# Three moves in the order of a fused attention and MLP block on one Trainium2 core

## The chip, the cores and the metric

The kernel runs on one NeuronCore of a Trainium2 chip. It is one launch that computes a whole residual block. The metric is the device time of one launch in microseconds (us); lower is better. In the rows of the profile PE is TensorE, DVE VectorE, ACT ScalarE, POOL GpSimd, and SP the engine whose queue issues nearly all transfers. Each engine works through its own list of instructions in order and waits for the others by semaphores.

## The reference

One sequence of 512 rows of width 2048 goes through an attention of 16 heads and an MLP of 8192 hidden columns, all in float32:

```python
h  = RMSNorm(x)
[qa|ka|va|qb|kb|vb|f] = h @ W_in
oa = stick-breaking attention (8 heads, strictly causal, no positions)
ob = forgetting attention (8 heads, causal, cumulative log-forget bias)
x  = x + concat(headnorm(oa), headnorm(ob)) @ W_out
x  = x + relu(RMSNorm(x) @ W_up)^2 @ W_down
y  = RMSNorm(x)
```

In the stick-breaking heads a query's weights are `exp(log_beta + rest)`, where `rest` is a running sum over keys from the right, which the kernel computes with scans.

## The kernel before, in words

**Numbers.** A float32 product is made of three products of shorter floats. `split` (L63) writes a high part (`wh`, `ah`, `fh`, `vh`, `ph`), on ACT, and the rest as a low part (`wl`, `al`, `fl`, `vl`, `pl`), on DVE: L65 and L66, or with a scale L68 and L69, which only V uses. A matmul then comes as high by high (L98), low by high (L99) and high by low (L100). So most of the work of ACT and DVE is splitting, and PE needs both parts of a piece soon after one another.

**Stages.** From 0 to about 628 us the projections and the heads; to about 795 us the output projection; to about 821 us its end, together with the turning of its result for the MLP; to about 1447 us the up-projection; then the down-projection, and the last norm to 2071 us.

**Output projection.** It is a Strassen-like scheme of seven products, numbered 1 to 7, over the two halves of each side. Their left sides are sums and differences of quarters of the heads' outputs (`mixed`). `left(p, j)` makes the part of product p's left side for two heads: for 5 a sum (L281), for 6 a difference (L283), for 2, 3 and 7 differences in place (L285, L287), and then a split. In the rows `al` with `ah` numbers 5298, 5320, 5322, 5318 and 5883 belongs to the products 1, 2, 5, 6 and 7. `out_piece` loads a piece of the weights (`wraw`, from `in_w_out` or from the prepared `tw`) and splits it; `out_product` multiplies it: 12 matmuls to a piece, half of them into each of two banks (`acca`, later `accc`). `add` (L595) adds the banks to the residual `r`. The first products start before the last two heads are done: their matmuls lie between those of the last V (`accv`), of two heads' outputs `o` (weights `ph`, `pl`, the transposes `pt` of `w`, times `vh`, `vl`) and of the sums of squares `ssq`. `first_outputs` (L563) issues this stretch. The list of each engine comes from a scheduler: the order of issue in the code is a priority, and `issue_after` tells it to hold something until an instruction has its place. V's parts have the highest priority there.

**The end of the output projection** is written out by hand for ACT and DVE. `out_step(j)` runs the 12 matmuls of piece j of product 4, with pieces split ahead (`ahead`). `turn_block` stores a finished half of the residual, turns it by eight transposes on PE (`tr`) and scales it on ACT into `h`; `to_sum`, `to_high` and `to_low` make of it the MLP's left sides (`fh`, `fl`, numbers 1 to 7 again: 6257, 6259, 6850, 6261, 6542, 6263, 6265). `squares` sums for the norm.

**Up-projection.** It goes through 32 units of 256 hidden columns (`Unit`); each again has seven products of 2.8 us on PE, and a product is `split_part` (its weights, `wh` and `wl`, or `wx`), `multiply` (16 matmuls) and `close`. A unit has three banks: A (`psa`) for 1, 6, 7 and 4, one after the other, B (`psb`) for 2, C (`psc`) for 5 and 3. After 1, 6 and 7 ACT copies bank A (L925, `s`) before the next product may go on in it; DVE adds B or C and forms the hidden columns, which are split (`st`) and stored (`ufd`). The units whose number leaves 2, 5 or 7 when divided by 8 load raw quarters and make their sums on DVE (L890 to L895). The loop takes one unit (`new`) together with the end of the one before (`old`):

```python
for i, (who, p) in enumerate(((new, 1), (old, 4), (new, 5), (new, 6), (old, 3), (new, 2), (new, 7))):
```

Units 0 and 1 stand ahead of the loop, with single loads (`more`) and products written out.

Of the kernel before, what the change touches and what calls it, by code (L numbers as in the profile page):

```python
# [8 lines left out]
F32 = mybir.dt.float32  # L9
F32R = mybir.dt.float32r  # L10
AF = mybir.ActivationFunctionType
ALU = mybir.AluOpType
# [28 lines left out]
def block_kernel(ctx, tc, x, g_attn, w_in, b_f, g_out_sb, g_out_fox, w_out, g_mlp, w_up, w_down, g_final, y):  # L41
    nc = tc.nc
    pe, act, dve, pool, sp = nc.tensor, nc.scalar, nc.vector, nc.gpsimd, nc.sync
# [14 lines left out]
    acc_cm = tc.tile_pool(name="acc", bufs=4, space=PSUM)  # L58
    acc = acc_cm.__enter__()

    lows, casts, loads, scaled = [None], [None], [None], [None]

    def split(hi, lo, src, scale=None):  # L63
        if scale is None:
            ins = casts[0] = act.copy(hi, src)  # L65
            lows[0] = dve.tensor_tensor(lo, src, hi.bitcast(F32), op=ALU.subtract)  # L66
        else:
            ins = act.mul(hi, src, scale)  # L68
            scaled[0] = dve.scalar_tensor_tensor(lo, src, scale, hi.bitcast(F32), op0=ALU.mult, op1=ALU.subtract)  # L69
        return ins  # L70

    more_parts, turn = [], [0]
# [83 lines left out]
    def out_rows(half, j, n):  # L156
        e = order[NH * half + 2 * j]
        return w_out[e * P:(e + 2) * P, n * NT:(n + 1) * NT].rearrange("(a p) c -> p a c", p=P)
# [50 lines left out]
    with tc.tile_pool(name="att", bufs=1, side="right") as at:  # L209
# [50 lines left out]
        def out_piece(p, c, j):  # L260

            src = out_rows(p > 1, j, 2 * c + (p == 3)) if p < 4 else tw[c][j][:, {5: 0, 7: 1, 6: 2, 4: 3}[p]]
            raw_turn[0] += 1
            i = raw_turn[0] % (3 + len(spares))
            raw = wp.tile([P, 2, NT], F32, tag="wraw", name="wraw") if i < 3 else spares[i - 3]()
            loads[0] = sp.dma_start(raw, src)
            hi, lo = (wp.tile([P, 2, NT], F32R, tag=f"w{q}", name=f"w{q}") for q in "hl")
            split(hi, lo, raw)
            return hi, lo

        def left_tile(p, pool_):
            LT[p] = tuple(pool_.tile([P, NH, 2 * P], F32R, tag=f"f{q}{LEFT_AT[p]}", name=f"a{q}{p}") for q in "hl")

        def left(p, j, k=1):

            m0, m1 = late["mixed"]
            ks = slice(2 * j, 2 * (j + k))
            a11, a21, a12, a22 = (m[:, ks, i:i + 2 * P] for m in (m0, m1) for i in (0, 2 * P))
            s = late["s"][j] if p in (5, 6, 3) else None
            if p == 5:  # L280
                dve.tensor_tensor(s, a21, a22, op=ALU.add)  # L281
            if p == 6:
                dve.tensor_tensor(s, s, a11, op=ALU.subtract)  # L283
            if p == 7:
                dve.tensor_tensor(a21, a11, a21, op=ALU.subtract)  # L285
            if p == 3:
                dve.tensor_tensor(a12, a12, s, op=ALU.subtract)  # L287
            if p == 1 and j < 2:
                out = [at.tile([P, 2, 2 * P], F32R, tag=f"a{q}{j}", name=f"a{q}1") for q in "hl"]
                late[1, j] = out  # L290
            else:
                out = [LT[p][q][:, ks] for q in range(2)]
            split(*out, {1: a11, 2: a12, 5: s, 6: s, 3: a12, 7: a21, 4: a22}[p])
# [203 lines left out]
        with tc.tile_pool(name="attp", bufs=1, space=PSUM) as atp:  # L497
# [46 lines left out]
            def residual(h, n, tiles):  # L544

                for t in range(2):
                    sp.dma_start(tiles[t], xq[:, 2 * h + t, n * NT:(n + 1) * NT])
                return tiles

            def two(c, dt=F32):  # L550
                return [up.tile([P, NT], dt, tag=f"u{p}{c}", name="r") for p in "hl"]

            def load_mixed(k):
                sp.dma_start(late["mixed"][k // NH][:, k % NH, :], md[order[k]])

            def before_outputs():
# [3 lines left out]
                left(1, 0)  # L560
                left(1, 1)

            def first_outputs():  # L563
                for k in (2 * NH - 4, 2 * NH - 3):
                    load_mixed(k)
                hp_cm.__exit__(None, None, None)
                pool_ = ctx.enter_context(tc.tile_pool(name="form", bufs=1, reuse_waits="tile"))
                FP.update((p, pool_) for p in (5, 6, 7, 4))
                spares.append(lambda: at.tile([P, 2, NT], F32, tag="raw4", name="wraw"))
                left_tile(1, pool_)  # L570
                with tc.issue_after(scaled[0].ins):
                    left(1, 2, 2)
                late["A"] = [[acc.tile([P, NT], F32, tag="acc", name="acca") for _ in range(2)] for c in range(2)]
                late[1, 1, 0], late[1, 1, 1] = (residual(0, 2 * c, two(2 + c)) for c in range(2))
                late["s"] = [w.rearrange("p (a b) -> p a b", a=2) for c in range(2) for w in two(c)]
                for p in (6, 2, 5):
                    left_tile(p, pool_)
                for c in range(2):
                    for j in range(4):
                        yield from out_product(late["A"][c], 1, c, [j], True, True)  # L580
                        if c == 0 and j < 3:
                            left(5, j)
                            left(6, j)
                    add(late[1, 1, c], late["A"][c])
                for c in range(2):
                    for j in range(3):
                        yield from out_product(late["A"][c], 6, c, [j], False, False)
                        if c == 0 and j == 0:
                            left(2, 0, 2)
                        if c == 0 and j == 1:  # L590
                            left(2, 2)

            def add(r, ps):
                for t in range(2):
                    dve.tensor_tensor(r[t], r[t], ps[t], op=ALU.add)  # L595
# [77 lines left out]
    def turn_block(h, n, r):  # L673

        for t in range(2):
            sp.dma_start(xd[n][:, 2 * h + t, :], r[t])
        for q in range(2):
            tr = trp.tile([P, 2, 2 * P], F32, tag="tr", name="tr1")
            for t in range(2):
                for i in range(2):  # L680
                    pe.transpose(tr[:, i, t * P:(t + 1) * P], r[t][:, (2 * q + i) * P:(2 * q + i + 1) * P], ident)
            for i in range(2):
                k = 2 * q + i
                act.mul(H[h][:, n, k, :], tr[:, i, :], g_up[:, 4 * n + k:4 * n + k + 1])
# [122 lines left out]
    r21 = [residual(1, 2 * c, two(2 + c)) for c in range(2)]  # L807
    for c in range(2):
        form_tile(5, c)
    for j in range(4):  # L810
# [8 lines left out]
        if j == 3:  # L819
            for b in range(2):  # L820
                squares(1, 2 * b + 1, r22[b])
    ahead = {j: out_piece(4, 1, j) for j in range(2)}
    M1 = []
    GROUPS = [(0, 3), (3, 3)] + [(u, 4) for u in range(6, NU - 2, 4)]
    ufd, at_unit = {}, {}
# [222 lines left out]

    out_step(0)
    add(r21[0], A[0])  # L1050
    ahead[2] = out_piece(4, 1, 2)
    out_step(1)
    ahead[3] = out_piece(4, 1, 3)
    u0, u1 = Unit(0), Unit(1)
    u0.more(5)
    turn_block(1, 0, r21[0])
    to_sum(5, 0)
    to_high(5, 0)
    to_sum(7, 0)
# [6 lines left out]
    to_low(7, 0)  # L1066
    out_step(2)
    u0.split_part(2)
    u0.more(7)
    to_high(6, 0)  # L1070
    to_low(6, 0)
    to_high(4, 0)
# [9 lines left out]
    u0.open_banks()  # L1082
    u1.open_banks()
    u1.split_part(1)
    u1.more(5)
    for n in (1, 3):
        to_high(3, n)
        to_low(3, n)
# [21 lines left out]
    to_high(4, 2)  # L1110
    to_low(4, 2)
    u1.multiply(2)
    u0.split_part(7)
    for n in (0, 2):
        to_high(3, n)
        to_low(3, n)
# [1 line left out]
    u1.close(2)  # L1118
    squares(1, 2, r21[1])
    u0.multiply(5)  # L1120
    u1.split_part(5)
    both_cm.__exit__(None, None, None)
    mixp_cm.__exit__(None, None, None)
    up_cm.__exit__(None, None, None)
# [9 lines left out]
    M1.append(mps.tile([P, 2, NT], F32, name="m1_0"))  # L1134
    u0.others()
    u1.others()
    for who, p in ((u0, 6), (u0, 7), (u1, 5), (u1, 6), (u0, 4), (u1, 7), (u0, 3)):
        who.product(p)
    more_parts.append(parts_hx)
    out_cm.__exit__(None, None, None)  # L1140
    old = u1
    for u in range(2, NU + 1):
        new = Unit(u) if u < NU else None
        if u == NU - 1:
            for p in ORDER:
                load_uf(p, GROUPS[0])
            b_first = load_b(GROUPS[0], 0)
        if new is None:
            second(1, b_first, 0, GROUPS[0][1], True)
        for i, (who, p) in enumerate(((new, 1), (old, 4), (new, 5), (new, 6), (old, 3), (new, 2), (new, 7))):  # L1150
            if who is None:
                continue
            who.product(p)
            if u == 3 and p == 6:
                v2 = cp.tile([P, TB], F32, name="v2")
                dve.tensor_reduce(v2, ss2, axis=mybir.AxisListType.X, op=ALU.add)
                dve.tensor_scalar(v2, v2, 1.0 / D, EPS, op0=ALU.mult, op1=ALU.add)
                ev = cp.tile([P, TB], F32, name="ev")
                dve.scalar_tensor_tensor(ev, v2, EPS, v2, op0=ALU.mult, op1=ALU.mult)
            if todo and u < NU - 1 and i in (0, 2, 4, 5):  # L1160
                store_form(*todo.pop(0))
            if p == 3 and who.u % 2 == 1 and who.u < NU - 2:
                todo += [(q, who.pair, who.u - 1) for q in A_ORDER]
        old = new
# [128 lines left out]
    for t in range(2, TB):  # L1293
        for n in range(4):
            ins = last_product(t, n, *banks[n % 2])
# [29 lines left out]
```

## Time and profile before

| | |
|---|---|
| three timed runs | 2073.26, 2077.16, 2079.03 us, median 2077.16 |
| the profiled execution's own time | 2072.78 us |
| its span (first to last instruction) | 2071.1 us |
| PE busy | 2036.7 us (98%), mean granted clock 0.996 |
| DVE busy | 1656.5 us (80%) |
| ACT busy | 1074.2 us (52%) |
| memory traffic | 373 MB read, 117 MB written, 237 GB/s |

The profiled execution is 0.5 us below the fastest of the three runs. A row of a timeline gives start, length, engine, line, operation, tiles written and read, shapes, how many alike, and in brackets how long the engine had been idle before and what ended that. A row of the table by windows gives for a stretch its length and then the busy time of PE, PE's weight loads, DVE, ACT and POOL, PE's granted clock (1.00 is full), the share of the transfer engines and GB/s. A matmul of 512 columns takes 0.39 us in the rows, but they overlap, and one starts every 0.2275 us.

### The profile page before, as it was taken

The page shows a single profiled execution, that of the slowest core. Times are in us where ns is not written, and L with a number is a line of the kernel's source. Part 1 is how long each engine was busy: PE and PEld are TensorE (multiplying, and loading weights), DVE is VectorE, ACT ScalarE, POOL GpSimd, SP SyncE. Part 2 cuts the span into 40 slices and gives each one's busy share as a digit, 9 for nine tenths or more (in the row PEclk, how much of TensorE's full clock was granted, in tenths as well). Part 3 has the DMA queues.
Part 4 walks back from the last instruction along what each step waited for, and adds up shares of the span by engine and source line. Part 5 has one row for each costly group of instructions (what it writes and reads, how often), then busy time and mean ns, then how long its engine had stood idle before and what let it go on. Part 6 is the DMA issues. An engine that isn't in the chain of part 4 may idle for free.

```text
span 2071.1 us, 26773 instructions
## 1 busy us (share of the span) xinstructions
PE 2036.7 (98%) x10188; PEld 1729.7 (84%) x10188; DVE 1656.5 (80%) x1866; ACT 1074.2 (52%) x1419; POOL 69.7 (3%) x73
## 2 busy tenths in 40 slices
PE   9999999999999999999999999999999999999998
PEld 8888888888887888888888888888888888888886
DVE  4767767768777778888888888887899989888886
ACT  5334334444546566666666666655744434443433
POOL 0000000001102000000000000000000000000003
PEclk9999999999999999999999999999999999999999
DMA  7888878888754876776877777777865764764722
GB/s 242 270 292 280 287 251 272 287 274 265 254 187 140 257 231 197 255 251 232 268 247 241 257 261 254 235 248 261 293 244 215 268 242 159 267 236 131 269 93 102
DMA packets 371728, 492.60 MB, mean 238 GB/s; under 512 B 12760, under 2 KB 258568, under 8 KB 362512
## 3 DMA queue, kind: packets, MB, share of 16 engines
q1 hardware_dynamic: 370640, 488.77, 71.2%
q10 hardware_dynamic: 960, 2.13, 0.3%
q8 instruction: 80, 1.31, 0.2%
q14 instruction: 48, 0.39, 0.1%
HBM read 373.39 MB, written 117.46 MB: 237 GB/s over the span
## 4 chain that ended last, share of the span: by engine, by line
PE 88%; DVE 5%; DMA 3%; ACT 2%; issue 1%; SPq 0%; ACTq 0%; DVEq 0%
PE psa L912 9%; PE accd L99 8%; PE accd L98 8%; PE accd L100 8%; PE accq L98 5%; PE accq L99 5%; PE accq L100 5%; PE psa L914 5%; PE psc L912 5%; PE accv L98 3%; PE accv L99 3%; PE accv L100 3%; PE psc L914 2%; PE psb L912 2%; DMA ufd<-st 2%
## 5 line engine op out<-in xcount | busy, mean ns | idle before, releaser
L65 ACT CAST wh<-wraw 128x1024 fp32r<-128x1024 f32 (+2 forms) x157 | 160.8, 1026 | 241.8 <-PE accq L99 113.4
L66 DVE TENSOR_TENSOR wl<-wraw,wh 128x1024 fp32r<-128x1024 f32 (+2 forms) x157 | 186.7, 1191 | 101.0 <-ACT wh L65 100.7
L65 ACT CAST wh<-wu 128x1024 fp32r<-128x1024 f32 x160 | 166.9, 1049 | 116.4 <-PE psa L912 48.0
L65 ACT CAST wh<-wd 128x1024 fp32r<-128x1024 f32 (+1 forms) x134 | 132.6, 999 | 181.4 <-PE accd L100 125.0
L66 DVE TENSOR_TENSOR wl<-wu,wh 128x1024 fp32r<-128x1024 f32 x160 | 194.5, 1221 | 27.8 <-ACT wh L65 21.8
L98 PE MATMUL accq<-hH,wh 128*128 128x512 f32 x512 | 201.1, 393 | 0.0
L100 PE MATMUL accq<-hH,wl 128*128 128x512 f32 x512 | 199.8, 390 | 0.0
L99 PE MATMUL accq<-hL,wh 128*128 128x512 f32 x512 | 199.6, 390 | 0.0
L66 DVE TENSOR_TENSOR wl<-wd,wh 128x1024 fp32r<-128x1024 f32 (+1 forms) x134 | 153.1, 1153 | 34.9 <-ACT wh L65 34.7
L98 PE MATMUL accd<-wh,uf 128*128 128x512 f32 x428 | 166.5, 389 | 0.1
L100 PE MATMUL accd<-wh,uf 128*128 128x512 f32 x428 | 166.5, 389 | 0.0
L99 PE MATMUL accd<-wl,uf 128*128 128x512 f32 x428 | 166.5, 389 | 0.0
L65 ACT CAST wx<-wd 128x1024 fp32r<-128x1024 f32 (+1 forms) x90 | 89.5, 1001 | 118.3 <-PE accd L100 79.1
L66 DVE TENSOR_TENSOR wx<-wd,wx 128x1024 fp32r<-128x1024 f32 (+1 forms) x90 | 103.1, 1155 | 21.7 <-ACT wx L65 21.6
L99 PE MATMUL accd<-wx,uf 128*128 128x512 f32 x292 | 114.0, 390 | 0.5 <-DVE wx L66 0.3
L98 PE MATMUL accd<-wx,uf 128*128 128x512 f32 x292 | 113.6, 389 | 0.2 <-ACT wx L65 0.2
L100 PE MATMUL accd<-wx,uf 128*128 128x512 f32 x292 | 113.6, 389 | 0.0
L100 PEld LDWEIGHTS accq<-hH,wl 128*128 128x128 f32 x512 | 96.1, 188 | 20.1
L99 PEld LDWEIGHTS accq<-hL,wh 128*128 128x128 f32 x512 | 96.2, 188 | 19.0
L98 PEld LDWEIGHTS accq<-hH,wh 128*128 128x128 f32 x512 | 96.2, 188 | 18.9
L1020 DVE TENSOR_TENSOR m<-m,accd 128x1024 f32<-128x1024 f32 x84 | 102.2, 1217 | 11.1 <-PE accd L100 11.1
L912 PE MATMUL psa<-fh,wh 128*128 128x512 f32 x392 | 106.6, 394 | 0.7 <-ACT s L925 0.7
(307 smaller groups left out, 4845.4 us busy)
## 6 DMA issues: line engine op xcount, KB each, us to landing
ufd<-st SPq DMA_DIRECT2D x98, 512.0 KB, 5.4
wd<-in_w_down_dram SPq DMA_DIRECT2D x48, 1024.0 KB, 7.2
wraw<-in_w_in_dram SPq DMA_DIRECT2D x84, 512.0 KB, 5.8
uf<-ufd SPq DMA_DIRECT2D x42, 1024.0 KB, 6.6
wu<-in_w_up_dram SPq DMA_DIRECT2D x66, 512.0 KB, 6.8
wu<-in_w_up_dram SPq DMA_DIRECT2D x32, 1024.0 KB, 8.5
sums<-in_w_up_dram SPq DMA_DIRECT2D x60, 512.0 KB, 5.3
td<-sums SPq DMA_DIRECT2D x20, 1536.0 KB, 5.8
```

The lines of the kernel that those rows point to most:

```text
L65: ins = casts[0] = act.copy(hi, src)
L66: lows[0] = dve.tensor_tensor(lo, src, hi.bitcast(F32), op=ALU.subtract)
L98: pe.matmul(out, sh, mh, start=first, stop=False, skip_group_check=True)
L99: pe.matmul(out, sh, ml, start=False, stop=False, skip_group_check=True)
L100: pe.matmul(out, sl, mh, start=False, stop=last, skip_group_check=True)
L912: pe.matmul(ps, hi[:, a, :], both, start=a == 0 and p in (1, 2, 5), stop=False, skip_group_check=True)
L914: pe.matmul(ps[:, :2 * P], lo[:, a, :], F[p][a // 4][:, a % 4, 0, :], start=False, stop=a == KC // 2 - 1, skip_group_check=True)
L1020: dve.tensor_tensor(M[p][:, :, db, :], M[p][:, :, db, :], ps, op=ALU.add)
```

## The change

Three things change; no instruction is added or removed, but many change places, since the lists follow the order of issue.

1. **Parts behind V's last.** `split` remembers both instructions of the last scaled split, ACT's and DVE's. `left(1, 2, 2)`, `left(5, j)`, `left(6, j)` and `left(2, ...)` in `first_outputs` are issued only after both; before, only `left(1, 2, 2)` was held back, and only behind DVE's.
2. **One turn in front of a piece.** `turn_block(1, 0, ...)` goes ahead of `out_step(1)` instead of behind it, and all four pieces are split ahead. Of units 0 and 1, product 5 of unit 1 and product 7 of unit 0 change places, with their loads and splits.
3. **In the loop**, the old unit's product 4 and the new unit's product 5 change places.

```diff
-    lows, casts, loads, scaled = [None], [None], [None], [None]
+    lows, casts, loads, scaled = [None], [None], [None], []
...
-            scaled[0] = dve.scalar_tensor_tensor(lo, src, scale, hi.bitcast(F32), op0=ALU.mult, op1=ALU.subtract)
+            scaled[:] = ins, dve.scalar_tensor_tensor(lo, src, scale, hi.bitcast(F32), op0=ALU.mult, op1=ALU.subtract)
...
+            def after_values(*what):
+                with tc.issue_after(scaled[0].ins), tc.issue_after(scaled[1].ins):
+                    left(*what)
...
-                with tc.issue_after(scaled[0].ins):
-                    left(1, 2, 2)
+                after_values(1, 2, 2)
...
-                            left(5, j)
-                            left(6, j)
+                            after_values(5, j)
+                            after_values(6, j)
...
-                            left(2, 0, 2)
+                            after_values(2, 0, 2)
...
-                            left(2, 2)
+                            after_values(2, 2)
...
-    ahead = {j: out_piece(4, 1, j) for j in range(2)}
+    ahead = {j: out_piece(4, 1, j) for j in range(3)}
...
     out_step(0)
     add(r21[0], A[0])
-    ahead[2] = out_piece(4, 1, 2)
+    ahead[3] = out_piece(4, 1, 3)
+    turn_block(1, 0, r21[0])
     out_step(1)
-    ahead[3] = out_piece(4, 1, 3)
     u0, u1 = Unit(0), Unit(1)
     u0.more(5)
-    turn_block(1, 0, r21[0])
...
-    u0.more(7)
+    u1.more(5)
...
-    u1.more(5)
+    u0.more(7)
...
-    u0.split_part(7)
+    u1.split_part(5)
...
-    u1.split_part(5)
+    u0.split_part(7)
...
-    for who, p in ((u0, 6), (u0, 7), (u1, 5), (u1, 6), (u0, 4), (u1, 7), (u0, 3)):
+    for who, p in ((u0, 6), (u1, 5), (u0, 7), (u1, 6), (u0, 4), (u1, 7), (u0, 3)):
...
-        for i, (who, p) in enumerate(((new, 1), (old, 4), (new, 5), (new, 6), (old, 3), (new, 2), (new, 7))):
+        for i, (who, p) in enumerate(((new, 1), (new, 5), (old, 4), (new, 6), (old, 3), (new, 2), (new, 7))):
```

Three lines more in the new code shift the line numbers: L595 becomes L598, L681 L684, L912 L915 and so on.

**DVE behind the scans of the last stick-breaking head** (where V's last low part `vl` is due). Before:

```order
L66 TENSOR_TENSOR al_5323<-r,ah_5322 128x512 x2
L401 TENSOR_TENSOR w<-s,w 128x1280
L66 TENSOR_TENSOR wl<-wraw,wh 128x1024
L66 TENSOR_TENSOR al_5323<-r,ah_5322 128x512
L283 TENSOR_TENSOR r<-r,mixed 128x512 x2
L66 TENSOR_TENSOR al_5321<-mixed,ah_5320 128x1024
L66 TENSOR_TENSOR al_5321<-mixed,ah_5320 128x512
L69 SCALAR_TENSOR_TENSOR vl<-accv,r1v,vh 128x256
L66 TENSOR_TENSOR al_5299<-mixed,ah_5298 128x1024
L66 TENSOR_TENSOR wl<-wraw,wh 128x1024 x2
```

And now:

```order
L66 TENSOR_TENSOR wl<-wraw,wh 128x1024
L69 SCALAR_TENSOR_TENSOR vl<-accv,r1v,vh 128x256
L281 TENSOR_TENSOR r<-mixed 128x512 x3
L66 TENSOR_TENSOR al_5299<-mixed,ah_5298 128x1024
L401 TENSOR_TENSOR w<-s,w 128x1280
L66 TENSOR_TENSOR al_5321<-mixed,ah_5320 128x1024
L66 TENSOR_TENSOR al_5321<-mixed,ah_5320 128x512
L285 TENSOR_TENSOR mixed<-mixed 128x2x256
L66 TENSOR_TENSOR wl<-wraw,wh 128x1024
L285 TENSOR_TENSOR mixed<-mixed 128x2x256
```

`vl` has gone from the tenth instruction to the second; the sums for product 5 (L281), which stood ahead of this stretch, and product 7's differences (L285) now stand behind it, and product 5's and 6's lows further back.

**DVE some 25 instructions further on**, at `pl<-pt`, the low part of the next head's weights; `al_5884` is product 7's left side. Before:

```order
L384 SCALAR_TENSOR_TENSOR ph<-ph,ra 128x512
L66 TENSOR_TENSOR wl<-wraw,wh 128x1024
L386 SCALAR_TENSOR_TENSOR mixed<-os,g_rest,ph 128x512
L66 TENSOR_TENSOR pl<-pt,ph 128x1280
L595 TENSOR_TENSOR r<-r,acca 128x512
L66 TENSOR_TENSOR wl<-wraw,wh 128x1024
L595 TENSOR_TENSOR r<-r,acca 128x512
L66 TENSOR_TENSOR al_5884<-mixed,ah_5883 128x512 x3
L66 TENSOR_TENSOR wl<-wraw,wh 128x1024
```

And now:

```order
L384 SCALAR_TENSOR_TENSOR ph<-ph,ra 128x512
L66 TENSOR_TENSOR wl<-wraw,wh 128x1024
L598 TENSOR_TENSOR r<-r,acca 128x512 x2
L66 TENSOR_TENSOR al_5884<-mixed,ah_5883 128x512 x3
L386 SCALAR_TENSOR_TENSOR mixed<-os,g_rest,ph 128x512
L66 TENSOR_TENSOR wl<-wraw,wh 128x1024
L66 TENSOR_TENSOR pl<-pt,ph 128x1280
```

The last head's norm (L386), and with it `pl<-pt`, has moved behind the adds of `r`, product 7's lows and one more weight piece. On ACT the cast `ph<-pt` has moved in the same way, behind product 7's casts and one more `wh`, and it waits for L386. On PE the order of this stretch has not changed.

**PE in the loop**, at unit 9 (product 7 is `fh_6265`, 5 is `fh_6542`, 2 is `fh_6259`, 4 is `fh_6261`). Before:

```order
L912 MATMUL psa<-fh_6265,wh 128x512 x4
L912 MATMUL psa<-fl_6266,wh 128x512 x4
L914 MATMUL psa<-fh_6265,wl 128x256 x4
L914 MATMUL psa<-fl_6266,wl 128x256 x4
L914 MATMUL psa<-fl_6258,wl 128x256 x4
L912 MATMUL psc<-fh_6542,wh 128x512 x4
L912 MATMUL psc<-fl_6543,wh 128x512 x4
L914 MATMUL psc<-fh_6542,wl 128x256 x4
L914 MATMUL psc<-fl_6543,wl 128x256 x4
L912 MATMUL psa<-fh_6261,wx 128x512 x4
```

And now:

```order
L917 MATMUL psa<-fl_6266,wl 128x256 x4
L915 MATMUL psc<-fh_6542,wx 128x512 x3
L917 MATMUL psa<-fh_6257,wl 128x256 x4
L917 MATMUL psa<-fl_6258,wl 128x256 x4
L915 MATMUL psc<-fh_6542,wx 128x512
L915 MATMUL psc<-fl_6543,wx 128x512 x4
L917 MATMUL psc<-fh_6542,wx 128x256 x4
L917 MATMUL psc<-fl_6543,wx 128x256 x4
L915 MATMUL psb<-fh_6259,wx 128x512 x4
L915 MATMUL psb<-fl_6260,wx 128x512 x4
L915 MATMUL psa<-fh_6261,wh 128x512 x4
```

Between the end of product 7 and the start of the old unit's 4 in bank A there was a product 5; now half of a product 2 lies there too. The scheduler had the order 1, 5, 4 already at this place; how far 7 and 4 stand apart now varies from unit to unit, with a pattern of eight units.

## Prediction

> **What bounds the kernel now.** I read the page's first part, then what TensorE (PE) waits for, then its clock in single windows, then the timelines of PE, VectorE (DVE) and ScalarE (ACT) at the three places that the change touches. First the busy time and PE's waits (total, times, longest).
>
> ```profile
> span 2071.1 us, 26773 instructions
> PE 2036.7 (98%) x10188; PEld 1729.7 (84%) x10188; DVE 1656.5 (80%) x1866; ACT 1074.2 (52%) x1419; POOL 69.7 (3%) x73
> PE psa L912 <- ACT s L925: 9.2, 6, 2.0
> PE o L100 <- DVE vl L69: 4.9, 1, 4.9
> PE psc L912 <- ACT wh L65: 1.8, 1, 1.8
> PE tr L681 <- DVE r L595: 1.6, 2, 1.5
> ```
>
> PE is 98% busy, so only its waits and its clock can be saved, and no matmul is removed or added. The four waits total 17.5 us: one in front of the head's output `o`, two at the turn of `r21`, the rest in the up-projection. Then the clock (fourth from the end of a row; the first figure after the comma is the stretch's length, the next PE's busy time).
>
> ```profile
> 639.46:642.87 3.41, 2.66 (x7) 1.96 (x8) 3.41 (x5) 1.84 (x3) 3.41 (x2) 0.50 0.00 1
> 642.87:646.28 3.41, 3.41 (x10) 2.64 (x9) 3.41 (x6) 0.88 (x2) 3.41 (x1) 0.50 0.70 220
> 1318.71:1322.12 3.41, 1.45 (x9) 1.07 (x8) 3.41 (x4) 2.31 (x3) 0.00 (x0) 1.00 0.42 158
> 1322.12:1325.53 3.41, 3.41 (x14) 3.03 (x13) 1.08 (x3) 1.04 (x1) 0.00 (x0) 0.50 0.95 307
> ```
>
> After the 4.85 us wait PE ran at half clock in two windows of 3.41 us: the rest of the one in which it resumed (640.21) and the next, to 646.28, 6.07 us, less the start of one matmul, and so 2.85 us lost. After a wait of 1.96 us inside one window it ran the next one at half clock, 1.6 us lost. So the change can take away at most 17.5 + 2.85 + 1.6 = 22 us, 1.1%.
>
> [...]
>
> **Part 1, the parts behind V's last.** Before, DVE behind the scans of `w`, and then PE (start, length, engine, line, tiles, shapes, count, and what ended the idle time ahead):
>
> ```profile
> 632.42 1.26 DVE L66 TENSOR_TENSOR al<-r,ah 128x512 fp32r<-128x512 f32 x2
> 633.61 1.48 DVE L401 TENSOR_TENSOR w<-s,w 128x1280 f32<-128x1280 f32 x1
> 635.01 1.21 DVE L66 TENSOR_TENSOR wl<-wraw,wh 128x1024 fp32r<-128x1024 f32 x1
> 636.14 0.68 DVE L66 TENSOR_TENSOR al<-r,ah 128x512 fp32r<-128x512 f32 x1
> ...
> 639.69 0.47 DVE L69 SCALAR_TENSOR_TENSOR vl<-accv,r1v,vh 128x256 fp32r<-128x256 f32 x1
> 640.08 1.21 DVE L66 TENSOR_TENSOR al<-mixed,ah 128x1024 fp32r<-128x1024 f32 x1
> 641.22 2.35 DVE L66 TENSOR_TENSOR wl<-wraw,wh 128x1024 fp32r<-128x1024 f32 x2
> 635.09 0.27 PE L99 MATMUL o<-pl,vh 128*128 128x128 f32 x1
> 640.21 0.48 PE L100 MATMUL o<-ph,vl 128*128 128x128 f32 x1 [4.85 <-DVE vl L69]
> ```
>
> DVE runs without a gap, so starts give the true cost: 0.60 for 512 columns, 1.14 for 1024, 1.40 for L401, 0.39 for `vl`. In the new order `vl` is second behind the scans: 632.42 + 1.14 + 0.39 = 634.0, and PE wants it at 635.36. The 4.85 us and their dip go at this place.
>
> What is late next: `al1`, behind three sums (L281), is done at 637.0 and wanted at 636.0, 1.1 us; the low part of the next piece (L401, two `al2` and one L285 stand ahead of it) at 641.9, wanted at 639.6, 2.4 us. Then nothing until the second head's output, whose low part `pl` from the transposes `pt` has been moved back:
>
> ```profile
> 652.77 1.23 DVE L66 TENSOR_TENSOR wl<-wraw,wh 128x1024 fp32r<-128x1024 f32 x1 [0.92 <-ACT wh L65]
> 654.68 0.69 DVE L383 SCALAR_TENSOR_TENSOR ph<-ssq,ph 128x512 f32<-128x512 f32 x1 [0.68 <-ACT ph L382]
> 657.15 0.75 DVE L386 SCALAR_TENSOR_TENSOR mixed<-os,g_rest,ph 128x512 f32<-128x512 f32 x1
> 657.98 1.23 ACT L65 CAST ph<-pt 128x1280 fp32r<-128x1280 f32 x1 [2.01 <-DVE mixed L386]
> 659.24 1.49 DVE L66 TENSOR_TENSOR pl<-pt,ph 128x1280 fp32r<-128x1280 f32 x1 [1.35 <-ACT ph L65]
> 660.65 0.68 DVE L595 TENSOR_TENSOR r<-r,acca 128x512 f32<-128x512 f32 x1
> 661.26 0.40 PE L98 MATMUL o<-ph,vh 128*128 128x512 f32 x1
> 661.50 0.39 PE L99 MATMUL o<-pl,vh 128*128 128x512 f32 x1
> ```
>
> Before, `ph` follows L386 on ACT, `pl` is ready 0.85 us before PE wants it (660.65 against 661.50), and DVE had 0.92 + 0.68 + 1.35 = 2.95 us to spare on the way. Now DVE does ahead of L386, from 632.42 on, 27 operations of 512 columns (16.2), 10 of 1024 (11.4), L401, `vl`, and L383, L384, L386 (2.1): 31.5 us, to 663.9. `ph` waits for L386 (it writes the tile that L386 reads), 664.0 to 665.1; `pl` runs to 666.7. The short count agrees: six sums and differences that were done before 629 (L281, L285), two adds of r, three `al7` and two weight lows now precede it, 11 x 0.60 + 2 x 1.14 = 8.9, less the 2.95 of slack, 5.9 later than 660.65. None of these waits on the way: the casts and matmuls that they need are done 2.5 us and more ahead.
>
> PE meanwhile needs from 635.4 six pieces of 12 matmuls (2.72 each, 0.2275 apart), the two sums of squares and ten transposes (1.5) and the two waits (3.5): it stands in front of `o` at 656.8, ahead of before by 4.4 us, and waits 8.4 us for `ph` and 1.2 us for `pl`. Its second matmul starts at 666.7 instead of 661.50: **+5.2 us**. A wait that long surely halves the clock: it ends at a random place of a window, on average 1.7 us before its end, and the next one follows as above: 5.1 us at half, **+2.6** (1.7 to 3.4). The earlier waits, and a possible dip after the 2.4 us, vanish in this one. Part 1: **+7.8 us**, bounds +6.2 to +9.3.
>
> The moved steps' other queues: ACT issues the exponential (L402) 2.7 us later, and POOL's two masks behind it start at 639.7.
>
> ```profile
> 637.07 12.60 POOL L348 TENSOR_SCALAR_AFFINE_SELECT w<-w 128x384 f32<-128x384 f32 x2 [7.39 <-ACT w L402]
> ```
>
> They took 12.6 us and ended with the first operations of DVE that read PSUM (`vl` at 639.69, L595 at 649.44). Now the first such one is the add at 647.65, and the transposes come at 650.4. If the masks missed it and waited for L383 at 653.9, `o` would be reached at 661: still covered by the wait to 665.2. SP issues three loads of pieces (`tw`) ahead of the loads of r that two of them followed; the pieces are split only behind `o`'s wait, and r is added later still, so the same wait covers both. Without that cover POOL's miss would cost 4 us.
>
> **Part 2, the turn in front of a piece.** The turn of `r21[0]` moves ahead of 12 matmuls, 2.72 us; what it produces is what DVE waits for.
>
> ```profile
> 794.55 1.03 PE L681 MATMUL tr<-ident,r 128*128 128x128 f32 x8
> 790.62 0.68 DVE L595 TENSOR_TENSOR r<-r,acca 128x512 f32<-128x512 f32 x1
> 796.78 0.69 DVE L720 TENSOR_TENSOR s<-h 128x512 f32<-128x512 f32 x1 [2.01 <-ACT h L684]
> 804.53 1.28 DVE L595 TENSOR_TENSOR r<-r,acca 128x512 f32<-128x512 f32 x2
> 805.26 0.44 PE L681 MATMUL tr<-ident,r 128*128 128x128 f32 x2 [1.46 <-DVE r L595]
> 805.86 0.87 PE L681 MATMUL tr<-ident,r 128*128 128x128 f32 x6 [0.16 <-DVE r L595]
> 821.38 1.20 PE L912 MATMUL psa<-fh,wh 128*128 128x512 f32 x4 [0.68 <-ACT s L925]
> ```
>
> The transposes come at 791.8 (their r is added by 791.3, the second row), ACT scales them 2 us earlier, DVE's 2.01 us gap closes, and the add at 804.53 falls to about 802.3, ahead of the next turn at 803.7: both waits go, −1.6. The wait of the last row goes too, −0.7: there product 7 of unit 0 followed 6 in the same bank and waited for the copy; now unit 1's product 5 lies between. The two swapped loads (`more`, one issue on SP each) take each other's place, and so do the products that use them, so neither gets less time. Part 2: **−2.3 us**; bounds −2.3 and +1.6 (the waits doubled, if the 0.5 us in front of the earlier turn does not hold).
>
> **Part 3, old 4 behind new 5.** Here PE waits for the copy of bank A behind product 7, needed by product 4.
>
> ```profile
> 998.17 2.00 ACT L65 CAST wh<-wu 128x1024 fp32r<-128x1024 f32 x2 [3.65 <-DVE wu L893]
> 1003.67 0.57 ACT L925 COPY s<-psa 128x512 f32<-128x512 f32 x1
> 1004.29 1.20 PE L912 MATMUL psa<-fh,wx 128*128 128x512 f32 x4 [1.67 <-ACT s L925]
> 1404.40 1.20 PE L912 MATMUL psa<-fh,wx 128*128 128x512 f32 x4 [1.46 <-ACT s L925]
> ```
>
> The wait is not the copy (0.57) but what ACT, in order, has ahead of it: at 998.17 a cast that waited 3.65 us for DVE, and five more. Six waits (9.2 − 0.68 + 1.75 = 10.3) and the dip at 1322 (1.6) are 11.9 us. In the new order PE does a whole 5 and mostly half of a 2 between 7 and 4 (5.1 us for unit 9, 3.3 before), but the pattern also leaves three units (11, 19, 27) with 1.2 us. I price what stays: at units 9, 17, 25 product 2's cast is now late, by 0.55 us each (PE there at 1001.9, cast at 1002.4), 1.65; unit 5, 0.7, half of such a wait; half of three waits of 1.46 at the thin places, 2.2. Left 4.5, gain **−7.4**. Bounds 0 (every wait moves elsewhere) and −11.9.
>
> **Sum.** +7.8 − 2.3 − 7.4 = −1.9 on a profiled execution of 2072.78 (span 2071.1 and 1.7 around it): 2070.9. That execution lies 4.4 us below the median of the runs (2077.16, range 2073.26 to 2079.03), so for a median I say 2075.3. 0.3%, 6.2 us, is about what this kernel's runs can tell from no change.
>
> **Rivals.** (a) *The parts do what they are for*: `pl` is in time and only 1.1 + 2.4 us wait. Then part 1 is −7.7 + 3.5 = −4.2, the sum −13.9, 2063.3. It needs DVE 9.6 us faster than its rows; only a backlog that I misread gives that. 0.14. (b) *Slower*: ACT's order, not the bank, sets the loop's waits. Each of the three thin places, with 1.2 us between 7 and 4, waits as long as the longest before, 2.0 us, and one more of them than before falls wholly into one window and halves the clock; the other waits stay. Three waits of 2.0 instead of those at units 9, 17 and 25 (5.3) and a dip of 1.6 make part 3 +2.3 instead of −7.4, the sum +7.8, 2085.0 for a median. It decides (more than 6.2 slower) once part 3 is above +0.7, that is the loop's waits and dips above 12.6 us. For it: ACT's casts wait for DVE, which is at 80%, and nothing takes work from either; against it: elsewhere the cover grows from 3.3 to 5.1 us. 0.16.
>
> **Chances.** Forecast 0.62, its own range −7 to +5, 2070 to 2082; (a) 0.14; (b) 0.16; what I have not seen, 0.08. Faster by over 0.3%: (a) 0.14, the lower edge of the forecast 0.06, the unseen 0.02: 0.22. Slower: (b) 0.12, the upper edge 0.03, the unseen 0.03: 0.18. Same 0.60. The range 2065 to 2084 takes in the forecast and the nearer part of both rivals, and leaves out most of (a), 0.12, and the far part of (b) and the unseen, 0.08.
>
> **What would show it.** In the profile after: a wait of `o` L98 on ACT `ph` of 8 us near 665 and half clock behind it, none on `vl`; two waits of `acca` of about 1 and 2.4 us near 637 and 642; no `tr` wait near 803; waits of `psa` on ACT in the loop of 4 to 5 us in sum. Wrong would be an `o` reached at 657 with `ph` there, or loop waits near 10 us.

## The result, and the profile after

The changed kernel takes 2086.03 us (median of five runs, 2082.75 to 2091.10), beside 2077.16 before (five runs, 2073.26 to 2079.03): ratio 1.0058, 95% interval 1.0043 to 1.0072. In a second set of runs (e5 below) it was 2084.19 beside 2075.28, 1.0052 (1.0039 to 1.0065). So it is slower by 11 to 12 us by the ratios (8.9 by the first two medians), above the upper end of my range (2084) and far from the 2075.3 that I forecast.

Below, *before* and *after* are the names of the two kernels. The profiled execution of after took 2088.44 us (span 2086.7), 15.7 more than before's. It lies 2.4 above its median, before's 4.4 below, so the traces show a larger difference than the medians. PE's waits of after:

```profile
PE psa L915 <- ACT s L928: 10.2, 7, 2.6
PE o L98 <- ACT ph L65: 6.3, 1, 6.3
PE psb L915 <- ACT wx L65: 6.2, 3, 2.3
PE acca L99 <- DVE wl L66: 2.1, 1, 2.1
PE acca L100 <- DVE al L66: 1.0, 1, 1.0
PE o L99 <- DVE pl L66: 0.7, 1, 0.7
```

The waits on `vl` and of `tr` are gone, as forecast. The head has four new ones. The loop's, forecast at 4.5 us, are 16.4: 10.2 in bank A, and 6.2 in a kind that before did not have, product 2 (`psb`) waiting for its weights' cast. Rows of PE with a wait in the head, then the clock there (columns as in the prediction, the granted clock fourth from the end):

```profile
636.42 0.50 PE L100 MATMUL acca<-wh,al 128*128 128x512 f32 x1 [1.02 <-DVE al L66]
641.30 0.65 PE L99 MATMUL acca<-wl,ah 128*128 128x512 f32 x1 [2.09 <-DVE wl L66]
664.46 0.80 PE L98 MATMUL o<-ph,vh 128*128 128x512 f32 x1 [6.26 <-ACT ph L65]
665.99 0.80 PE L99 MATMUL o<-pl,vh 128*128 128x512 f32 x1 [0.73 <-DVE pl L66]
```

```profile
641.48:644.89 3.41, 3.41 (x9) 2.63 (x10) 3.41 (x6) 0.00 (x0) 3.41 (x1) 0.50 0.64 184
665.37:668.78 3.41, 2.79 (x10) 2.60 (x10) 0.56 (x1) 0.00 (x0) 0.00 (x0) 0.50 0.00 0
668.78:672.19 3.41, 3.41 (x11) 2.78 (x10) 0.69 (x1) 1.83 (x3) 0.00 (x0) 0.50 0.02 5
672.19:675.60 3.41, 3.41 (x16) 2.78 (x15) 0.94 (x1) 1.05 (x1) 0.00 (x0) 1.00 0.00 0
```

Each of the four waits is where the prediction put it. The first matmul of unit 0, behind the head, starts at 808.40 where it stood at 800.88 before: +7.5, part 1. From there to the first matmul of the down-projection (`accd`, 1448.00 before, 1463.18 now) is the stretch that I call the loop: 654.8 us in place of 647.1. In that +7.7 part 2's −2.3 is contained, so by these two traces part 3 costs +10.0: 6.2 of waits (16.4 for 10.2) and three windows of half clock, 1.7 us each, for one of 1.6. The remaining 0.5 us lie behind the loop. One trace is not much for such a sum. A second execution of after (e5) has a loop of only 647.5 us, with 12.6 us of waits and one window of half clock, so how much of the loss is part 3's is better read from the times of the experiments.

What makes the loop's waits is seen on ACT. At unit 9 of after, first ACT, then PE, then the queue SP:

```profile
992.39 1.14 ACT L65 CAST st<-c 128x512 fp32r<-128x512 f32 x2 [2.34 <-issue]
994.55 0.62 ACT L65 CAST st<-c 128x512 fp32r<-128x512 f32 x1 [1.02 <-DMA ufd<-st]
...
1002.60 0.62 ACT L65 CAST st<-c 128x512 fp32r<-128x512 f32 x1 [3.49 <-DMA ufd<-st]
1003.12 2.00 ACT L65 CAST wh<-wu 128x1024 fp32r<-128x1024 f32 x2
1005.02 1.06 ACT L949 ACTIVATE c<-c 128x1024 f32<-128x1024 f32 x1
1006.11 1.06 ACT L950 ACTIVATE c<-c 128x1024 f32<-128x1024 f32 x1
1007.08 1.03 ACT L65 CAST wx<-wu 128x1024 fp32r<-128x1024 f32 x1
1008.01 0.58 ACT L928 COPY s<-psa 128x512 f32<-128x512 f32 x1
```

```profile
1008.16 1.20 PE L915 MATMUL psb<-fh,wx 128*128 128x512 f32 x4 [1.78 <-ACT wx L65]
```

```profile
992.16 3.47 SPq L870 DMA_DIRECT2D wu<-td  x1
995.72 8.82 SPq L957 DMA_DIRECT2D ufd<-st  x4
```

`CAST st<-c` is `store_form`: a form of the finished hidden units is cast into one of three tiles (`st`, of the same buffers as `wraw`) and stored to memory (`ufd`). Three forms stand at 992.39 to 995.17. The fourth needs the first one's tile, whose store leaves SP at 995.72, behind a load that held the queue for 3.47 us, and lands at 1002.50, 6.8 us later (the median of these stores is 5.7). So ACT stands still for 3.49 us with casts behind it that are ready, and the last of these, `wx`, is what PE waits for at 1008.16. At unit 11, where I had seen a thin place in bank A, it is the same chain:

```profile
1041.03 1.05 ACT L65 CAST wh<-wu 128x1024 fp32r<-128x1024 f32 x1 [1.30 <-issue]
1045.22 0.62 ACT L65 CAST st<-c 128x512 fp32r<-128x512 f32 x1 [3.13 <-DMA ufd<-st]
...
1048.73 0.58 ACT L928 COPY s<-psa 128x512 f32<-128x512 f32 x1
```

```profile
1049.36 1.19 PE L915 MATMUL psa<-fh,wh 128*128 128x512 f32 x4 [1.89 <-ACT s L928]
```

ACT's waits for these stores were in the profile of before as well (total, times, longest; the first row is before, the second after). The prediction has no term for them: it goes from PE's waits one step back, and no further.

```profile
ACT st L65 <- DMA ufd<-st: 41.4, 21, 6.9
```

```profile
ACT st L65 <- DMA ufd<-st: 50.5, 21, 4.5
```

What differs is where they stand. At unit 9 before, the fourth form stood behind the two weight casts and the first activation that follow it here, and came at 1001.04 without a wait; in the new order it stands ahead of them. ACT at unit 9 before:

```profile
990.89 1.66 ACT L65 CAST st<-c 128x512 fp32r<-128x512 f32 x3
...
998.17 2.00 ACT L65 CAST wh<-wu 128x1024 fp32r<-128x1024 f32 x2 [3.65 <-DVE wu L893]
1000.08 1.05 ACT L946 ACTIVATE c<-c 128x1024 f32<-128x1024 f32 x1
1001.04 0.60 ACT L65 CAST st<-c 128x512 fp32r<-128x512 f32 x1
```

### The profile page after: what moved, and what is told of

Same layout as the page of the kernel before. It is cut to its first block, busy times and chain, and to the rows that moved or that the text cites. A ratio compares the mean times of both kernels' runs of the same rounds, so it can differ in the third digit from the quotient of the medians.

```text
span 2086.7 us, 26752 instructions
## 1 busy us (share of the span) xinstructions
PE 2043.2 (98%) x10188; PEld 1733.1 (83%) x10188; DVE 1657.0 (79%) x1866; ACT 1071.2 (51%) x1419; POOL 64.7 (3%) x73
## 4 chain that ended last, share of the span: by engine, by line
PE 84%; DVE 6%; DMA 5%; ACT 2%; issue 2%; SPq 0%; DVEq 0%; ACTq 0%
PE psa L915 8%; PE accd L99 8%; PE accd L98 8%; PE accd L100 8%; PE accq L98 5%; PE accq L99 5%; PE accq L100 5%; PE psa L917 4%; PE psc L915 4%; DMA ufd<-st 3%; PE accv L98 3%; PE accv L99 3%; PE accv L100 3%; PE psb L915 2%; PE psc L917 2%
## 5 line engine op out<-in xcount | busy, mean ns | idle before, releaser
L915 PE MATMUL psa<-fh,wh 128*128 128x512 f32 x392 | 108.6, 399 | 10.2 <-ACT s L928 10.2
L1023 DVE TENSOR_TENSOR m<-m,accd 128x1024 f32<-128x1024 f32 x84 | 102.2, 1216 | 11.1 <-PE accd L100 10.9
```

The lines of the kernel that those rows point to most:

```text
L915: pe.matmul(ps, hi[:, a, :], both, start=a == 0 and p in (1, 2, 5), stop=False, skip_group_check=True)
L1023: dve.tensor_tensor(M[p][:, :, db, :], M[p][:, :, db, :], ps, op=ALU.add)
```

## The experiments

The theory (A) has three parts: part 1 costs what its trace shows; part 2 gains; part 3 costs because forms that stand close together hold ACT up. Rivals: the distance in bank A makes the waits whatever the stores do (the forecast's step); or one part carries all. The table gives the ratio to before as measured beside it (95% interval), the length of the loop in the profiled execution, the sum of PE's waits in it of 0.15 us and more behind 860 us, and ACT's waits of these casts (`st`) for their stores, as the profile names them, all in us.

| run | what it is | ratio | loop | PE waits | ACT waits for stores |
|---|---|---|---|---|---|
| before | | 1 | 647.1 | 10.2 | 41.4 |
| e1 | part 1 | 1.0023 (1.0012 to 1.0034) | 645.4 | 8.5 | 40.6 |
| e2 | part 2 | 0.9975 (0.9962 to 0.9987) | 643.3 | 8.5 | 45.1 |
| e3 | part 3 | 1.0022 (1.0012 to 1.0031) | 652.5 | 14.2 | 52.7 |
| e6 | parts 2, 3 | 1.0024 (1.0013 to 1.0034) | 650.0 | 15.3 | 41.5 |
| e5 | after, again | 1.0052 (1.0039 to 1.0065) | 647.5 | 12.6 | 36.0 |
| e4 | after, stores from POOL | 1.0002 (0.9989 to 1.0014) | 640.4 | 7.0 | 39.7 |
| e7 | parts 2, 3, POOL | 0.9979 (0.9969 to 0.9988) | 643.5 | 10.2 | 40.5 |
| e8 | part 2, POOL | 0.9953 (0.9941 to 0.9965) | 638.6 | 5.7 | 21.2 |
| e9 | parts 2, 3, spread | 0.9936 (0.9924 to 0.9947) | 635.3 | 2.4 | 13.0 |
| e14 | part 2, spread | 0.9939 (0.9926 to 0.9952) | 636.5 | 4.6 | 11.0 |
| e10 | parts 2, 3, spread, POOL | 0.9941 (0.9928 to 0.9954) | 635.3 | 2.1 | 10.4 |
| e11 | part 2, spread, POOL | 0.9931 (0.9919 to 0.9942) | 635.2 | 3.4 | 5.3 |
| e13 | after, spread | 0.9966 (0.9954 to 0.9978) | 635.5 | 2.9 | 11.1 |
| e12 | part 2, part 1 in part | 0.9981 (0.9971 to 0.9992) | 645.6 | 11.2 | 46.9 |

In e5 and e6 the last column is too low. Three waits of the fourth form in e5 (11.4 us) and two in e6 (8.1) stand there under an operation of DVE that happened to end just then. A store landed 0.10 us ahead of each of these casts, as ahead of after's. With them it is 47.4 and 49.6, so the four traces with part 3 and the stores as they were (after, e3, e5, e6) have 47 to 53 us, and those without part 3 (before, e1, e2, e12) 41 to 47.

**The parts by themselves (e1, e2, e3).** Each takes over the lines of its part in the diff and leaves the others as before. Expected of part 1, part 2 and part 3:

> The kernel before with part 1 alone (the parts behind V's last). Theory A (the costs lie where the trace of after shows them): +7.5 us against before, about 2084.7; waits of acca of 1.0 and 2.1 us near 637 and 642, of o on ph of 6.3 us, and the loop's waits as before, 9 to 11 us. Rival B (the parts cost little by themselves, and the loss is all in the loop, which starts later): within 3 us of before. Rival C (the parts carry the whole loss): +9 or more.

> The kernel before with part 2 alone (the turn in front of a piece, and the two products exchanged). Theory A: -2.3 us, about 2074.9; no wait of tr near 805 and no wait of 0.7 us near 821. Rival B: the waits come back behind the shifted adds and the time stays, 2077.

> The kernel before with part 3 alone (in the loop, old 4 behind new 5). Theory A: slower, +4 to +10 us (2081 to 2087): waits of PE in the loop of 15 to 17 us in place of 10, and two or three windows of half clock in place of one, since ACT's casts of the stored forms now stand ahead of casts that are ready, and wait for their tiles' stores. Rival B, the forecast's step: the longer way between products 7 and 4 in bank A takes the waits away, -7 us (2070). Rival C: the waits only change places, within 2 us of before.

Part 1 measured +4.8 us (0.0023 of 2075; interval 2.5 to 7.1), under A's 7.5. In its trace the first product of unit 0 starts at 807.29, 6.4 later than before, with the waits where they were expected; the loop then happened to wait 1.7 us less. Part 2 measured −5.2, more than the −2.3: the waits of `tr` are gone, and that execution had no window of half clock in the loop. Its one new wait, 1.43 us for a weight cast at 828.12, I had costed at nothing. Part 3 alone is slower, +4.6 us, with waits of the new kind (14.2 us in the loop and one window of half clock, a little less than A's 15 to 17 and two or three); rival B, my forecast's step, is out.

**Whether the parts add up (e5, e6).** The whole kernel again, beside the kernel without part 1.

> The kernel after, once more, on the chip and beside the runs of the other three of this call. Parts 1, 2 and 3 alone gave +4.7, -5.2 and +4.5 us (ratios 1.0023, 0.9975, 1.0022). Theory A (the three add up): +4 us, ratio 1.002. Rival B (in the whole kernel the loop waits longer than in part 3 alone, 16.4 us against 14.2, and has more windows of half clock): +9 to +12 us again, ratio 1.0043 to 1.006.

> The kernel after without part 1 (parts 2 and 3 together on the kernel before). Theory A (the parts add up): -1 us, ratio 0.9997. Rival B (part 2 loses its gain in the new loop, or the loop's waits grow behind it): +4 to +7 us. The distance to the whole kernel in this call is part 1: 5 to 7.5 us by theory A, under 3 us if the loop took its wait up.

They don't: 4.8 − 5.2 + 4.6 is 4.2, the whole 10.8. Part 1 adds +5.8 to parts 2 and 3 (1.0052 less 1.0024), much as by itself. Part 3 adds +10.2 to part 2 (1.0024 less 0.9975), where alone it cost 4.6. The two pairs were measured on two chips, and the intervals of the two differences almost touch; whether and why part 2 makes part 3 dearer I leave open.

**The stores on another queue (e4, e7, e8).** In `store_form`, on after, on parts 2 and 3, and on part 2:

```diff
-            sp.dma_start(ufd[g0][p][:, :, j0:j0 + 2, :], st.bitcast(F32))
+            pool.dma_start(ufd[g0][p][:, :, j0:j0 + 2, :], st.bitcast(F32))
...
-                sp.dma_start(ufd[g][p][:, :, j, :], st[:, :, i, :].bitcast(F32))
+                pool.dma_start(ufd[g][p][:, :, j, :], st[:, :, i, :].bitcast(F32))
```

> The kernel after, with one change: the stores of the hidden forms (ufd) are issued from POOL's queue in place of SP's, where they stand behind loads that wait for a free buffer. Theory A (a store that leaves late frees its tile late, ACT's next cast into that tile waits, and all that stands behind it on ACT, the copy of bank A and the weights' casts, is late for PE): ACT's waits for these stores fall from 50 us to under 20, PE's waits in the loop from 16 to 8 or less, 2076 to 2080. Rival B (the distance between products 7 and 4 and the order of the casts make the waits, whatever the stores do): PE's waits in the loop stay at 14 to 17 us, 2084 to 2088. Rival C: POOL issues stores more slowly than SP, ACT's waits grow, and the time goes above 2088.

> As the last (parts 2 and 3 without part 1), with the stores of the hidden forms issued from POOL's queue. Theory A (the stores' place behind blocked loads on SP's queue makes the loop's waits): PE's waits in the loop 6 to 8 us in place of 14 to 16, and 6 to 9 us faster than the run without it, about 2068. Rival B (it was the changed order of ACT in that other run, or chance): within 2 us of the run without it.

> Part 2 alone with the stores issued from POOL's queue, old 4 ahead of new 5 as before. Theory A (the stores set the loop's waits in the old order as well): PE's waits in the loop fall from 8.5 us in part 2 alone to 4 to 6, about 2068, 0.3% faster than before. Rival B (in the old order the waits come from the distance in bank A between products 7 and 4, whatever the stores do): 8 to 10 us in the loop, 2071. Whether this or the last is the faster shows what part 3 is worth once the stores are out of the way: by the forecast's step part 3 gains.

All three are faster than on SP's queue, by 10 us (e4 against e5), 9 (e7 against e6) and 5 (e8 against e2), and PE's waits fall to 7.0, 10.2 and 5.7 us. But the mechanism was only half met: ACT's waits for the stores stay at 40 us in e4 and e7, where under 20 was expected of e4, and e7's 10.2 us of PE's waits lie above the 6 to 8 expected. Nor were the stores quicker: from POOL's queue they took 6.4 us to land (the median in e4 and e7), from SP's 5.7 (the median in after). So an earlier store is not shown to be what frees ACT; and in e4 and e7 the order on ACT also changed at units 9, 17 and 25 (one or both activations now ahead of the fourth form), so these runs mix two causes. With the old order of 4 and 5 (e8) it is 5.4 us faster than with the new one (e7), again against the forecast's step.

**The forms spread out (e9, e10, e11, e13, e14).** Only the order changes, and no instruction: seven forms of a pair evenly over two units, one behind every second product, and each held behind the cast of the product just issued. Before, the seven take eleven products, and ACT's list has up to three of them in a row (990.89 above) and a fourth a few casts behind.

```diff
-            if todo and u < NU - 1 and i in (0, 2, 4, 5):
-                store_form(*todo.pop(0))
+            if todo and u < NU - 1 and i in ((0, 2, 4, 6), (1, 3, 5))[u % 2]:
+                with tc.issue_after(casts[0].ins):
+                    store_form(*todo.pop(0))
```

> Parts 2 and 3 together, the stores on SP's queue as in the kernel, but the seven forms of a pair of units spread evenly over two units (one behind every second product, each held behind that product's cast on ACT; before, four of them follow one another within three products). Theory A (ACT reaches a form's cast before its tile's store is done, and ready work behind it waits): ACT's waits for stores fall from 41 us to under 25, PE's waits in the loop from 15 us to 6 to 10, and the time by 5 to 9 us against parts 2 and 3 as they are, to 2071 to 2075. Rival B (the distance in bank A and the weights' casts make the waits): PE's waits stay at 13 to 16 us, 2078 to 2081.

> As the last, and the stores issued from POOL's queue. Theory A: PE's waits in the loop 4 to 7 us (10 with the stores close together), 2066 to 2069. Rival B: no better than without the spreading, 2070.

> Part 2 alone, old 4 ahead of new 5, the stores from POOL's queue and spread as in the last. Theory A with the order of 4 and 5 worth nothing by itself: as the last within 2 us, 2065 to 2069, since once ACT is not held up neither order waits long. Rival B (the new order of 4 and 5 is worse by itself): 2062 to 2065, 3 us or more below the last. Rival C, the forecast's step (the longer way in bank A gains): 3 us or more above the last.

> The whole kernel after, and only the forms spread evenly over two units (on SP's queue). Theory A (the loop's loss is the bunched forms, and what is then left of the change is part 1's cost and part 2's gain): part 1's 5 to 8 us above parts 2 and 3 with the spreading (0.9936), so ratio 0.996 to 0.9975, about 2067; waits in the loop under 5 us. Rival B (part 1 costs more, because the loop meets the stores in another phase): loop waits of 8 us or more, ratio 0.999 to 1.001.

> Part 2 alone with old 4 ahead of new 5, and the forms spread evenly, on SP's queue; the fourth corner beside part 2 (0.9975), parts 2 and 3 (1.0024) and parts 2 and 3 with the spreading (0.9936). Theory A (the order of 4 and 5 is worth nothing of its own, it only set how many forms stood close together on ACT): 0.992 to 0.995, loop waits under 5 us. Rival B (the old order is worse by its short way in bank A, the forecast's step): 0.996 or more, waits of psa of 1 to 2 us at units 9, 17 and 25 and at others. Rival C (the new order is worse by itself): 0.991 or less.

e9 is 18 us faster than the same two parts without it (0.9936 for 1.0024), twice the most that I expected of it (e10 and e11, too, are 4 to 5 us below the range that I gave). Its ACT at unit 9 and ACT's waits for stores:

```profile
984.92 0.61 ACT L65 CAST st<-c 128x512 fp32r<-128x512 f32 x1
...
988.49 0.61 ACT L65 CAST st<-c 128x512 fp32r<-128x512 f32 x1
...
992.63 1.06 ACT L946 ACTIVATE c<-c 128x1024 f32<-128x1024 f32 x1
...
994.53 1.05 ACT L947 ACTIVATE c<-c 128x1024 f32<-128x1024 f32 x1
995.49 0.60 ACT L65 CAST st<-c 128x512 fp32r<-128x512 f32 x1
...
996.48 1.05 ACT L65 CAST wx<-wu 128x1024 fp32r<-128x1024 f32 x1
```

```profile
ACT st L65 <- DMA ufd<-st: 13.0, 7, 2.8
```

The forms stand 3.6 and 7.0 us apart, none of these three waits, and `wx` is cast behind them, after one copy, without a gap. Of the loop's 15 us of waits 2.4 are left, and no window of half clock. The edit moves other instructions too, since all lists follow the order of issue; a fourth tile, which would take the waits away and leave the order, was not tried. What settles the cause is e9 together with the other corners, all beside part 2. On SP's queue the old and the new order of 4 and 5 differ by 10 us with the forms close together (0.9975, 1.0024), and not measurably with the forms spread (e14 0.9939, e9 0.9936). On POOL's queue, spread, they do not either (0.9931, 0.9941). So the order of 4 and 5 is worth nothing by itself; it acted through the places that the forms took on ACT. In the old order the waits of bank A that I had meant to save are still there when nothing else disturbs, and small: 1.10 us at 997.37, 0.23 at 1154.13 and 0.51 at 1313.02 in e14, with two more of this kind, 1.19 at 1175.59 and 1.36 at 1392.67. With the forms spread the queue is worth nothing either. And after with the forms spread (e13) lies 6.2 us above e9: that is part 1, in a loop that no longer waits.

**Part 1 in part (e12).** Part 2, and of part 1 only `left(1, 2, 2)` and the two `left(2, ...)` behind V's last.

> Part 2, and of part 1 only left(1, 2, 2) and the two left(2, ...) held behind V's last parts; products 5 and 6 keep their old places. V's last low part comes fourth behind the scans, in time, and the head's pl stands behind 26.0 us of DVE's work by its rows in place of 33.7. Theory A (DVE's backlog sets when o's second matmul can start): o waits 3 to 5 us near 657 to 661, its second matmul starts near 660.7, 0.8 us earlier than before, and half clock behind it costs 2.6: about 2 us slower than part 2 alone, ratio to before 0.9975 to 0.999. Rival B (the parts do what they are for once pl isn't pushed back): 4 us faster than part 2 alone, 2067. Rival C (all of part 1's loss comes with any held part): ratio 1.000 or more.

PE's rows with a wait in the head of e12:

```profile
635.84 0.33 PE L100 MATMUL o<-ph,vl 128*128 128x128 f32 x1 [0.52 <-DVE vl L69]
638.98 0.51 PE L100 MATMUL acca<-wh,al 128*128 128x512 f32 x1 [2.29 <-DVE al L66]
660.01 0.51 PE L99 MATMUL o<-pl,vh 128*128 128x512 f32 x1 [1.45 <-DVE pl L66]
```

1.2 us slower than part 2 alone by the ratios, as A had it, with intervals that overlap. V's wait falls from 4.85 to 0.52 and comes back as 2.29 and 1.45 (3 to 5 expected of the last); `o`'s second matmul starts at 660.01, 1.5 us earlier than before (0.8 expected). The half clock expected behind it did not come; one window of it follows the 2.29. So holding products 5 and 6 back made most of part 1's loss: it pushed the start of `pl` from 658.48 (e12) to 664.44 (after), behind some 32 us of DVE's work from the scans on in place of some 26. Without that there was nothing to win here either: `al` and `pl`, further back in DVE's list, are late in `vl`'s place.

**A version faster than both.** e9, e11 and e14 are all 12 to 15 us below before; the lowest median is e11's, 2060.06 us beside 2073.9. The smallest edit with that gain is part 2 with the forms spread (e14, 2062.09 beside 2074.73).

## Why the prediction was wrong

**Part 1, +7.8: right in the mechanism and in the trace.** The trace has +7.5 (e1's 6.4); by the ratios it is 4.8 to 6.2, at and below the low end of my bounds. The start of unit 0 scatters by itself: it lies between 798.81 and 800.95 in the ten traces with the old head, and between 807.29 and 808.73 in the five with the new one. Why the times show less than these 8 us is open. Point by point: `al` 1.02 (forecast 1.1), `wl` 2.09 (2.4), `o`'s second matmul at 665.99 (666.7). The wait on `ph` was 6.26 and not 8.4, mostly because behind the 2.09 us there was a window of half clock (641.48 to 644.89, granted 0.50), so that PE came 1.7 us later to the wait that I had let swallow it; in e5 and e13, which have no such window, the wait is 7.87 and 7.88. Behind `o`, half clock lasted to 672.19, 7.0 us of work, and PE lost 3.5 us where I had 2.6.

**Part 2, −2.3: right in the trace**, where the three waits named are gone; by its own comparison (e2) −5.2, interval −7.9 to −2.7, which leaves my −2.3 out. The loop of that execution waited 1.7 us less and had no half clock; whether part 2 does that or chance is not shown.

**Part 3, −7.4: wrong, and it is the step that failed**, in the words of the prediction: "I price what stays". Of 4.5 us left I had 1.65 for product 2's late cast at units 9, 17 and 25; it was 1.78 + 2.29 + 2.14 = 6.2. I had 2.2 for the thin places at units 11, 19 and 27; they were 1.89 + 1.83 + 2.64 = 6.4. Two waits at units 21 and 29, 2.12 and 0.96, were not foreseen, nor three windows of half clock. The gain that I took, the longer way in bank A, shows only as 1 to 2 us less of waits in the traces with the forms spread (2.4 in e9 for 4.6 in e14, 2.1 in e10 for 3.4 in e11) and not in the times, because bank A was never what held most of those waits. ACT's order was, as I wrote, but behind ACT I followed one instance to a cast that waited for DVE and took it for all. The 41.4 us of waits for `ufd` stores, which the new order moved ahead of casts that PE needs, had no term.

Rival (b), at 0.16, came out by size: 2.0 us at each thin place and one more window of half clock, 2085.0; measured 2086.0. That the two lie so near is in part luck. Its premise that ACT sets the loop's waits was right. Its reason was not: ACT waited for stores there, not for DVE, and its "the other waits stay" missed the new kind at units 9, 17 and 25. Of the signs that I had named for being wrong, loop waits near 10 us came true, with 16.4 (12.6 in e5).

## What to carry over

When an in-order engine releases the waits that you mean to remove, list that engine's own waits before you price a new order: here 41 us of waits on ACT for its three store tiles were in the profile, and a new order decides only what is queued behind them. Ask of each moved operation which recycled buffer it needs, how long that buffer's store takes, and how many such operations now stand within that time; spreading them out was worth 7 us in the old order of the products and 18 in the new, and that order by itself nothing. And a bound for "every wait moves elsewhere" that ends at zero is too kind: waits can grow, here PE's in the loop from 10.2 to 16.4 us.

## What was not expected of the hardware

In the trace of after, whether half clock followed a wait of about 2 us went with where the wait fell. Its half-clock stretches up to the end of the loop begin at 641.48, 661.96, 1170.55, 1334.39 and 1378.76: 6, 155, 203 and 216 times 3.413 us behind the first, and on this raster they also end. A wait of 2.29 us that lay, but for 0.05 us, inside one window of the raster was followed by a window of half clock, as was the one of 2.14 before 1334.18:

```profile
1167.12:1170.53 3.41, 1.15 (x5) 0.98 (x6) 1.93 (x3) 2.66 (x4) 0.00 (x0) 1.00 0.66 176
1170.53:1173.94 3.41, 3.41 (x10) 2.62 (x9) 2.12 (x4) 0.00 (x0) 0.00 (x0) 0.50 0.63 243
1251.03:1254.44 3.41, 1.29 (x8) 0.94 (x7) 2.77 (x4) 3.41 (x6) 0.00 (x0) 1.00 0.43 162
1254.44:1257.85 3.41, 3.41 (x20) 2.96 (x19) 2.62 (x3) 2.68 (x5) 0.00 (x0) 1.00 0.91 261
```

The one of 2.12 at 1253.57, which a boundary of the raster (1252.47) cuts in two, 1.01 and 1.10 us, was not (its two rows are cut off the raster, so that the whole wait lies in the first), and neither was one of 2.68 us at 1157.27 in e8, cut into 0.90 and 1.78. In the traces of before and after, from 100 us on to 12 us before the end, seven windows of the raster at full clock were followed by half clock; PE was idle in them for 3.41, 3.41, 2.39, 2.24, 2.14, 2.09 and 1.96 us. The longest idle time that was not followed by it is 1.75 us (1356.26 of before). No threshold is shown by that: of two windows with 1.86 us, one was followed by half clock (e3) and one was not (e6), and in e1 one with 1.62 us among the transposes `tr` was followed by it, while at the same place in before (803.30), with 1.62 us too, the clock stayed at 1.00. And where the clock was already halved, a window with 0.62 us without work (665.37 to 668.78 above) was followed by another at half, while windows with 0.50 in e4 and 0.52 in e6 were not. Twelve runs of e6, with 15.3 us of waits in the loop, lie within 10.3 us, five of e9, with 2.4, within 3.1; whether half clock makes that difference no run shows.
